# NaN-ignoring maximum of 65,536 rows: one in-place ScalarE pass in place of keys and write-backs

## The chip, the cores and the metric

The kernel runs on one core of one Trainium2 chip. The metric is device time in microseconds. A core has five engines with instruction queues of their own: TensorE (PE in the profile), VectorE (DVE), ScalarE (ACT), GpSimd (POOL) and SyncE (SP), which here only issues transfers. Transfers between the device memory and the on-chip memory (128 partitions) run on 16 DMA engines beside them. Engines wait for each other through semaphores.

## The reference

```python
def setup_inputs():
    batch, seq, dim = 32, 2048, 2048
    x = np.random.randn(batch, seq, dim).astype(np.float32)
    mask = np.random.rand(batch, seq, dim) < 0.1
    x[mask] = np.nan
    return {"x": x, "axis": -1}

def reference(x, axis):
    return np.nanmax(x, axis=axis).astype(np.float32)
```

There are 65,536 rows of 2,048 float32 values, 536.87 MB in all; a tenth of the values are NaN. Each row gives the largest of its values that are not NaN (NaN, if all are).

## The kernel before

Each of the 128 partitions holds 512 rows. The list `TILES` cuts them into 74 tiles; an entry gives the tile's loads, the pieces of ScalarE's pass and the widths of VectorE's reductions, in quarter rows of 512 values. The bulk of the list are tiles of 28 quarters (7 rows, 56 KB in each partition, 7,168 KB in all) fetched by one load; towards the end a tile comes in more and smaller loads. Three buffers `xt` are used in turn, and a load into a buffer waits for the last reduction of the tile that was in it. The loads are issued by SP, in order, each with one of 14 semaphores in turn.

[...]

- ScalarE reads the upper half-words of a piece of the tile (every second 16-bit element of `xt`) and writes a dense 16-bit key into one of three buffers `kt`: a `Prelu` of 32639.25 minus the half-word, whose slope on the negative side sends NaN to a key that comes back as minus infinity.
- The write-back computes 32639 minus the key and puts it into the upper half-words of `xt`, again every second 16-bit element. GpSimd does most pieces (a positive number in `TILES`), ScalarE the rest (a negative one).

VectorE then takes the maximum of each row from `xt` (`tensor_reduce` in float32; line 239 in the profile). A reduction may cover part of a row; its result is left in the tile, in the element before the next part, which takes it in. At the end `find` (VectorE) and `find_late` (GpSimd) turn rows that are still minus infinity into NaN, and SP stores the results of six groups of rows in six transfers.

The order of work on each engine is the order in which the program calls `order.add`, which attaches to each instruction the semaphore waits that its engine has not yet seen. The lines of the profile are those of the helpers: L222 is every activation of ScalarE, L232 every write-back of GpSimd, L239 every reduction, L316 the loads, L461 the stores, L245 `find`. The key pass and ScalarE's write-back share line 222, so they are told apart by what they read and write: `kt<-xt` is the key pass, `xt<-kt` the write-back.

Of the kernel before, what the change touches and what calls it, by code (L numbers as in the profile page):

```python
# [7 lines left out]
D = 2048  # L9

Q = D // 4

TILES = (
    [([4], [4], [4])]
    + [([28], [7, 9, 12], [16, 12])] * 7
    + [([28], [9, 12, -7], [8, 20])]
    + [([28], [7, 9, 12], [16, 12])] * 7  # L20
    + [([28], [9, 12, -7], [8, 20])]
    + [([28], [7, 9, 12], [16, 12])] * 7
    + [([28], [9, 12, -7], [8, 20])]
    + [([28], [7, 9, 12], [16, 12])] * 7
    + [([28], [9, 12, -7], [8, 20])]
    + [([28], [7, 9, 12], [16, 12])] * 7
    + [([28], [9, 12, -7], [8, 20])]
    + [([28], [7, 9, 12], [16, 12])] * 7
    + [([28], [6, 10, 12], [16, 12])] * 3
    + [([28], [7, 9, 12], [16, 12])]  # L30
    + [([28], [6, 10, 12], [16, 12])] * 3
    + [([28], [7, 9, 12], [12, 16])] * 2
    + [([28], [7, 10, 11], [12, 16])]
    + [([28], [6, 10, 12], [16, 12])] * 3
# [13 lines left out]
)  # L48

GROUPS = [TILES[i : i + 15] for i in range(0, 60, 15)] + [TILES[60:73], TILES[73:]]  # L50


FLAGGED = (3, 5)
LATE = 4

APART = (70, 71, 72, 73)
WIDE = 7
BUFS = 3

KEYS = 3 * D  # L60
NKEYS = 3

LEAD = 128

# [4 lines left out]
TOP = 0x7F7F  # L69
NAN = 0x7FC0  # L70
LOW = -128

EDGE = TOP + 0.25

LEAST = -(2.0**128 - 2.0**104)


def total(pieces):
    return sum(sum(map(abs, p)) if isinstance(p, tuple) else abs(p) for p in pieces)


def joints(pieces, reds):

    flat = []
    at = 0  # L90
    for step, parts in enumerate(pieces):
        for c in parts if isinstance(parts, tuple) else (parts,):

            flat.append((at, at + abs(c), c < 0, step + isinstance(c, float)))
            at += abs(c)
    needs = []
    done = 0
    for n in reds:
        over = [i for i, (a, b, _, _) in enumerate(flat) if a < done + n and b > done]
        done += n  # L100
        pools = [i for i in over if not flat[i][2]]
        backs = [i for i in over if flat[i][2]]
        if pools and backs and flat[pools[-1]][3] > flat[backs[-1]][3]:
            backs = []
        needs.append(pools[-1:] + backs[-1:])
    pairs = {}
    for need in needs:
        if len(need) == 2 and all(sum(i in n for n in needs) == 1 for i in need):
            for i in need:
                pairs[i] = tuple(need)  # L110
    return pairs


class Order:

# [18 lines left out]
    def unseen(self, who, deps):  # L134
        seen = self.seen.setdefault(who, {})
        return [(s, v) for s, v in deps if seen.get(s, 0) < v]

    def needed(self, who, deps):

        seen = self.seen.setdefault(who, {})  # L140
        want = {}
        for s, v in self.unseen(who, deps):
            want[s] = max(want.get(s, 0), v)
# [10 lines left out]
    def add(self, who, engine, issue, deps, lane=None, step=1, joint=False):  # L154
# [12 lines left out]
        past = self.past.get((name, event[1] - step), {}) if joint else {}  # L167
        self.past[event] = {**past, **self.seen[who], name: event[1]}
        return event
# [3 lines left out]
def kernel(  # L173
# [6 lines left out]

# [13 lines left out]
    ACT = mybir.ActivationFunctionType  # L194

# [7 lines left out]
    rows = [sum(sum(loads) for loads, _, _ in g) * Q // D for g in GROUPS]  # L203
    assert R == P * sum(rows)

    sing = ctx.enter_context(tc.tile_pool(name="sing", bufs=1))

    scalars = sing.tile([P, LEAD // 4], f32, name="scalars")
    warm = scalars[:, 1:2]
    xts = [sing.tile([P, WIDE * D], i32, name=f"xt{i}") for i in range(BUFS)]  # L210
    kts = [sing.tile([P, KEYS], u16, name=f"kt{i}") for i in range(NKEYS)]
    accs = sing.tile([P, sum(rows)], f32, name="acc")
    late = sing.tile([P, rows[LATE]], i32, name="late")

    with tc.tile_critical():  # L215
        order = Order(nc)

        def act(deps, pair=None, **kw):
            return order.add(
                "act",  # L220
                nc.scalar,
                lambda: nc.scalar.activation(**kw),  # L222
                deps,
                lane=pair,
                joint=pair is not None,
            )

        def pool(deps, pair=None, **kw):
            return order.add(
                "pool",  # L230
                nc.gpsimd,
                lambda: nc.gpsimd.tensor_scalar(**kw),  # L232
                deps,
                lane=pair,
                joint=pair is not None,
            )
# [4 lines left out]
        def find(deps, acc):  # L241
            return order.add(
                "dve",
                nc.vector,
                lambda: nc.vector.scalar_tensor_tensor(  # L245
                    out=acc,
                    in0=acc,
                    scalar=LEAST,
                    in1=acc,
                    op0=ALU.is_ge,  # L250
                    op1=ALU.mult,
                ),
                deps,
            )

        def find_late(deps, acc, none):
            e = order.add(
                "pool",
                nc.gpsimd,
                lambda: nc.gpsimd.tensor_scalar(  # L260
                    out=none,
                    in0=acc,
                    scalar1=LEAST,
                    scalar2=float(0x00400000),
                    op0=ALU.is_lt,
                    op1=ALU.mult,
                ),
                deps,
            )
            bits = acc.bitcast(i32)  # L270
            return order.add(
                "pool",
                nc.gpsimd,
                lambda: nc.gpsimd.tensor_tensor(out=bits, in0=bits, in1=none, op=ALU.add),  # L274
                [e],
            )

        e_warm = order.add("dve", nc.vector, lambda: nc.vector.memset(warm, 1.0), [])  # L278
        act([e_warm], out=warm, in_=warm, func=ACT.Prelu, alpha=0.5)

        free = [[] for _ in range(BUFS)]
        kfree = [[] for _ in range(NKEYS)]
        clock = 0

        def last(uses):

            return list({back: e for back, _, e in sorted(uses, key=lambda u: u[1])}.values())

        key = 0
        used = KEYS  # L290
        number = 0
        lanes = [[] for _ in range(LANES)]
        turn = 0
        stores = []
        ready = []
        flagged = 0
        r0 = 0
        for gi, (s, g) in enumerate(zip(rows, GROUPS)):
# [3 lines left out]
            first = sum(rows[:gi])  # L302
            acc = accs[:, first : first + s]
            base = 0
            for loads, pieces, reds in g:
                assert sum(loads) == total(pieces) == sum(reds)
                xt, before = xts[number % BUFS], free[number % BUFS]
                number += 1
                landed = []
                at = 0  # L310
                for c in loads:
                    c *= Q
# [191 lines left out]
```

## Time and profile before

| What | Value |
|---|---|
| Median of 3 runs | 1252.61 us (1252.61 to 1252.66) |
| Span of the profiled execution | 1250.7 us |
| VectorE busy | 1111.4 us, 179 instructions |
| ScalarE busy | 965.6 us, 273 instructions |
| GpSimd busy | 1168.5 us, 242 instructions |
| Read from device memory | 536.87 MB, 429 GB/s over the span |
| Loads | 105, of which 61 of 7,168 KB |
| ScalarE's key pass (`kt<-xt`) | 913.4 us in 247 instructions |
| ScalarE's write-back (`xt<-kt`) | 52.8 us in 24 |
| GpSimd's write-back (`xt<-kt`) | 1167.4 us in 236 |
| VectorE's reductions | 1109.2 us in 176 |

The profiled execution is one run of the program under the hardware profiler; the median comes from runs without it and is 1.9 us longer than the profile's span. In a list of groups, a row gives the line, the engine and the operation, then what it writes and reads with the shape (partitions by elements per partition), the count, the busy time in us and the mean of one in ns, and last the idle time of the engine just before these instructions and what ended it. In a timeline a row gives the start and the length in us; several like instructions in a row are merged, and the count stands behind the x. The DMA row gives the busy share of the 16 DMA engines in tenths, in 40 equal slices of the span or of the window; the GB/s row what they moved in each.

### The profile page before, as it was taken

To read this page: it belongs to the slowest core of one execution; us is meant where nothing else is said; L and a number is where in the kernel's file an instruction comes from. 1 tells how busy PE (TensorE), PEld (TensorE's weight loads), DVE (VectorE), ACT (ScalarE), POOL (GpSimd) and SP (SyncE) were. 2 spreads that over 40 slices of the span, in tenths; PEclk is the share of its full clock that TensorE was granted. 3 is DMA by queue.
4 is the path that set the end of the run, shared out by engine and by line. 5 is a ranking of instruction groups with operands and counts; after the bars stand their busy time and mean duration, and the time that the engine had idled before them with its cause. 6 is when DMAs were issued, how large, how long until landed. Compare 5 with 4: busy or idle time off the path is not lost.

```text
span 1250.7 us, 891 instructions
## 1 busy us (share of the span) xinstructions
DVE 1111.4 (89%) x179; ACT 965.6 (77%) x273; POOL 1168.5 (93%) x242
## 2 busy tenths in 40 slices
DVE  0888989888889888898988888998888899999999
ACT  3777887778777877788777877777777778999997
POOL 2999989998999899998999899999999999989998
DMA  9999999999999999999999999999999999999997
GB/s 415 440 418 433 440 440 438 413 440 440 440 433 418 440 440 438 429 424 440 440 436 424 431 440 438 436 424 433 440 438 435 422 436 436 425 434 429 431 428 301
DMA packets 15991, 537.20 MB, mean 430 GB/s; under 512 B 2544, under 2 KB 2544, under 8 KB 3568
## 3 DMA queue, kind: packets, MB, share of 16 engines
q1 hardware_dynamic: 15984, 537.14, 99.4%
q14 instruction: 7, 0.06, 0.0%
HBM read 536.87 MB, written 0.26 MB: 429 GB/s over the span
## 4 chain that ended last, share of the span: by engine, by line
DMA 40%; DVE 29%; POOL 22%; ACT 9%; issue 1%; SPq 0%
DMA xt<-in_x_dram 40%; DVE acc L239 29%; POOL xt L232 22%; ACT kt L222 8%; ACT xt L222 1%; SPq L316 0%; DVE acc L245 0%; SPq L499 0%; SPq L215 0%
## 5 line engine op out<-in xcount | busy, mean ns | idle before, releaser
L232 POOL TENSOR_SCALAR xt<-kt 128x3584 int16<-128x3584 uint16 (+11 forms) x236 | 1167.4, 4947 | 77.6 <-ACT kt L222 63.9
L239 DVE TENSOR_REDUCE acc<-xt 128x3 f32<-128x6144 f32 (+4 forms) x175 | 1107.5, 6379 | 135.6 <-POOL xt L232 128.1
L222 ACT ACTIVATE kt<-xt 128x3584 uint16<-128x3584 int16 (+9 forms) x247 | 913.4, 3734 | 278.0 <-DMA xt<-in_x_dram 257.9
L222 ACT ACTIVATE xt<-kt 128x512 int16<-128x512 uint16 (+6 forms) x24 | 52.8, 2202 | 0.7
L245 DVE SCALAR_TENSOR_TENSOR acc<-acc 128x414 f32<-128x414 f32 (+1 forms) x2 | 2.2, 1111 | 0.1
L222 ACT ACT_TABLE_LOAD x1 | 1.3, 1283 | 0.9 <-SPq L215 0.9
L239 DVE TENSOR_REDUCE xt<-xt 128x1 f32<-128x1536 f32 x1 | 1.7, 1743 | 0.0
L278 DVE MEMSET scalars<- 128x1 f32 x1 | 0.1, 59 | 1.0 <-SPq L215 1.0
L260 POOL TENSOR_SCALAR late<-acc 128x91 int32<-128x91 f32 x1 | 0.5, 549 | 0.1
L274 POOL TENSOR_TENSOR acc<-acc,late 128x91 int32<-128x91 int32 x1 | 0.3, 341 | 0.1
L485 POOL MEMSET const-float32-0.0<- 128x1 f32 x1 | 0.1, 98 | 0.2 <-issue 0.2
L222 ACT ACTIVATE scalars<-scalars 128x1 f32<-128x1 f32 x1 | 0.2, 203 | 0.0
L485 POOL MEMSET const-bfloat16-1.0<- 128x1 bf16 x1 | 0.1, 101 | 0.0
L485 POOL MEMSET const-uint8-127<- 128x1 uint8 x1 | 0.1, 101 | 0.0
L485 POOL MEMSET const-float32-1.0<- 128x1 f32 x1 | 0.1, 98 | 0.0
## 6 DMA issues: line engine op xcount, KB each, us to landing
xt<-in_x_dram SPq DMA_DIRECT2D x61, 7168.0 KB, 22.6
xt<-in_x_dram SPq DMA_DIRECT2D x2, 5120.0 KB, 17.4
xt<-in_x_dram SPq DMA_DIRECT2D x3, 2816.0 KB, 22.7
xt<-in_x_dram SPq DMA_DIRECT2D x4, 2048.0 KB, 22.3
xt<-in_x_dram SPq DMA_DIRECT2D x5, 1536.0 KB, 29.1
xt<-in_x_dram SPq DMA_DIRECT2D x2, 3584.0 KB, 24.8
xt<-in_x_dram SPq DMA_DIRECT2D x6, 1024.0 KB, 26.8
xt<-in_x_dram SPq DMA_DIRECT2D x3, 1792.0 KB, 30.1
```

What stands on the lines that cost most here:

```text
L222: lambda: nc.scalar.activation(**kw),
L232: lambda: nc.gpsimd.tensor_scalar(**kw),
L239: return order.add("dve", nc.vector, lambda: do(**kw), deps)
L245: lambda: nc.vector.scalar_tensor_tensor(out=acc, in0=acc, scalar=LEAST, in1=acc, op0=ALU.is_ge, op1=ALU.mult,),
L260: lambda: nc.gpsimd.tensor_scalar(out=none, in0=acc, scalar1=LEAST, scalar2=float(0x00400000), op0=ALU.is_lt, op1=ALU.mult,),
L274: lambda: nc.gpsimd.tensor_tensor(out=bits, in0=bits, in1=none, op=ALU.add),
L278: e_warm = order.add("dve", nc.vector, lambda: nc.vector.memset(warm, 1.0), [])
L485: nc = _bacc.Bacc("TRN2", target_bir_lowering=False, num_devices=1)
```

## The change

The two steps become one. ScalarE reads the upper half-words h of a piece of `xt` as signed 16-bit numbers and writes max(2h - 32640, 0), as an unsigned 16-bit number, into the same place. In this code NaN becomes the half-word of minus zero and every value under 2 becomes a number under the smallest normal one (2 to the power of -126), while values from 2 up keep their order, with the lower half-words as they are. VectorE takes the maxima as before. A decode of the upper half-words of the results, (code + 32640) / 2, gives the values back.

A row with no value of 2 or more has no normal number in the result. Such rows are marked on GpSimd (`mark`), the marks are summed (ScalarE, and TensorE over the partitions), the sum is loaded into a register on VectorE and ScalarE, and if it isn't zero, a general path (`general`) computes everything anew. The inputs here don't lead into it.

There are no keys, no buffers `kt` and no write-backs any more; GpSimd only marks and decodes. The tiles are cut anew, in units of 256 values: 52 tiles of 64 units (8 rows, 64 KB in each partition) in one load each, then 15 tiles of 24 to 64 units with loads that shrink to 3 to 5 units, 98 loads in all. A load of 24 units or more is passed over by ScalarE in two pieces, split at a row. The rows form two groups (501 and 11 rows in each partition) in place of six, so there are two stores.

```diff
-TILES = (
-    [([4], [4], [4])]
-    + [([28], [7, 9, 12], [16, 12])] * 7
...
+U = 256
+ROW = D // U
+TILES = [[64]] * 52 + [
+    [56],
+    [56],
+    [40],
+    [48],
+    [32, 32],
+    [40],
+    [26, 30],
+    [32],
+    [27, 29],
+    [16, 24],
+    [15, 17, 16, 16],
+    [15, 14, 12, 13, 10],
+    [11, 11, 10, 8, 8, 8, 8],
+    [8, 8, 7, 7, 6, 6, 6, 6, 5, 5],
+    [3, 5, 5, 3, 4, 4],
+]
...
+def pieces(load, at):
+    if load >= 3 * ROW:
+        half = (at + load // 2) // ROW * ROW - at
+        return [half, load - half]
+    return [load]
...
+        def decode(where, a, b, deps):
+            add, do = (dve, nc.vector) if where == "dve" else (pool, nc.gpsimd)
+            return add(
                 deps,
+                do.tensor_scalar,
+                out=halves[:, a:b],
+                in0=halves[:, a:b],
+                scalar1=float(INF),
+                scalar2=0.5,
+                op0=ALU.add,
+                op1=ALU.mult,
             )
...
+                if number == len(TILES) - 1:
+                    e_early = total(late[:, 0:1], low, [e_low])
...
-                        act(
-                            [e],
-                            name(i),
-                            out=xt[:, a:b].bitcast(i16)[:, 1::2],
-                            in_=kp,
-                            func=ACT.Copy,
-                            bias=float(TOP),
-                            scale=-1.0,
...
+                    for piece in pieces(load, at):
+                        span = xt[:, at * U : (at + piece) * U]
+                        e_clean = act(
                             [e],
+                            out=span.bitcast(u16)[:, 1::2],
+                            in_=span.bitcast(i16)[:, 1::2],
+                            func=ACT.Relu,
+                            bias=float(-INF),
+                            scale=2.0,
                         )
...
+                e = mark(late[:, 1:s], accs[:, first : S - 1], [e_before])
+                e_dec = decode("pool", first, S - 1, [e_before, e])
+                e = mark(late[:, s : s + 1], last_part, [e_part])
+                e_sums = order.add(
+                    "pe",
+                    nc.tensor,
+                    lambda: nc.tensor.matmul(sums, lhsT=ones, rhs=late, start=True, stop=True),
+                    [e, e_early, e_ones],
+                )
+                e = decode("dve", S - 1, S, [e_max])
...
+        e_sum = total(flag, sums, [e_sums])
+        order.wait("act", nc.scalar, [e_sum])
+        order.wait("dve", nc.vector, [e_sum])
+        lows = nc.values_load(
+            flag.bitcast(i32),
+            engines=[ENG.DVE, ENG.Activation],
+            skip_runtime_bounds_check_because="it is only compared with zero",
+        )
+        with nc.If(lows != 0):
+            general(nc, order, ended, xr, of, xts, accs, small)
```

More of the change, by code (lines that the diff above doesn't have):

```diff
@@ L50 @@
[L50 to L57, printed above, removed]
+U = 256
[17 more added lines that the diff above has]
+]
+SPLIT = len(TILES) - 2
+WIDE = 8
@@ L58 @@
 BUFS = 3
-KEYS = 3 * D
-NKEYS = 3
-LEAD = 128
 LANES = 14
[L69 to L111, printed above, removed]
+INF = 0x7F80
@@ L114 @@
+NORMAL = 2.0**-126
 class Order:
@@ L152, in needed, with wait, add @@
         return list(want.items())
-    def add(self, who, engine, issue, deps, lane=None, step=1, joint=False):
+    def wait(self, who, engine, deps):
+        for s, v in self.needed(who, deps):
+            engine.wait_ge(self.sems[s], v)
+    def add(self, who, engine, issue, deps, lane=None, step=1):
         want = self.needed(who, deps)
@@ L202 @@
     of = out.bitcast(i32).flatten_outer_dims().rearrange("r c -> (r c)")
-    rows = [sum(sum(loads) for loads, _, _ in g) * Q // D for g in GROUPS]
-    assert R == P * sum(rows)
+    groups = [TILES[:SPLIT], TILES[SPLIT:]]
+    rows = [sum(map(sum, g)) // ROW for g in groups]
+    S = sum(rows)
+    assert R == P * S
+    assert all(sum(t) % ROW == 0 and sum(t) <= WIDE * ROW for t in TILES)
     sing = ctx.enter_context(tc.tile_pool(name="sing", bufs=1))
-    scalars = sing.tile([P, LEAD // 4], f32, name="scalars")
@@ L209 @@
-    warm = scalars[:, 1:2]
+    psum = ctx.enter_context(tc.tile_pool(name="psum", bufs=1, space=bass.MemoryType.PSUM))
     xts = [sing.tile([P, WIDE * D], i32, name=f"xt{i}") for i in range(BUFS)]
-    kts = [sing.tile([P, KEYS], u16, name=f"kt{i}") for i in range(NKEYS)]
-    accs = sing.tile([P, sum(rows)], f32, name="acc")
-    late = sing.tile([P, rows[LATE]], i32, name="late")
+    accs = sing.tile([P, S], f32, name="acc")
+    low = sing.tile([P, rows[0]], f32, name="low")
+    late = sing.tile([P, 1 + rows[1]], f32, name="late")
@@ L215 @@
+    small = sing.tile([P, 64], f32, name="small")
+    sums = psum.tile([1, 1 + rows[1]], f32, name="sums")
+    ones, warm, flag = small[:, 0:1], small[:, 1:2], small[0:1, 2:3]
+    halves = accs.bitcast(u16)[:, 1::2]
     with tc.tile_critical():
         order = Order(nc)
[L218 to L236, printed above, removed]
+        def act(deps, **kw):
+            return order.add("act", nc.scalar, lambda: nc.scalar.activation(**kw), deps)
         def dve(deps, do, **kw):
             return order.add("dve", nc.vector, lambda: do(**kw), deps)
[L241 to L252, printed above, removed]
-                deps,
-            )
@@ L278, with pool @@
-        e_warm = order.add("dve", nc.vector, lambda: nc.vector.memset(warm, 1.0), [])
-        act([e_warm], out=warm, in_=warm, func=ACT.Prelu, alpha=0.5)
-        free = [[] for _ in range(BUFS)]
[L282 to L291, printed above, removed]
+        def pool(deps, do, **kw):
+            return order.add("pool", nc.gpsimd, lambda: do(**kw), deps)
@@ L301 @@
             r0 += P * s
-            first = sum(rows[:gi])
-            acc = accs[:, first : first + s]
             base = 0
-            for loads, pieces, reds in g:
-                assert sum(loads) == total(pieces) == sum(reds)
+            for loads in g:
                 xt, before = xts[number % BUFS], free[number % BUFS]
-                number += 1
-                landed = []
                 at = 0
-                for c in loads:
-                    c *= Q
+                part = []
+                if number == len(TILES) - 1:
+                    e_early = total(late[:, 0:1], low, [e_low])
+                for load in loads:
                     e = order.add(
@@ L324 @@
                     turn = (turn + 1) % LANES
-                    landed.append((at, at + c, e))
-                    at += c
-                clean = []
-                after = []
-                at = done = 0
-                reds = [n * Q for n in reds]
-                part = []
-                held = []
-                pairs = {}
-                if number not in APART:
-                    pairs = joints(pieces, [n // Q for n in reds])
-                flat = sum((p if isinstance(p, tuple) else (p,) for p in pieces), ())
@@ L441 @@
-                            after.append(e)
-                free[(number - 1) % BUFS] = after[-1:]
-                base += at
-            stores.append((og, acc.bitcast(i32)))
-            if gi == LATE:
-                late_after = after
-            elif gi not in FLAGGED:
-                continue
-            lo, flagged = flagged, first + s
-            if gi == LATE:
-                late_acc = accs[:, lo:flagged]
-            else:
-                e = find(after, accs[:, lo:flagged])
-                ready += [e] * (gi + 1 - len(ready))
@@ L455 @@
-            if gi == len(GROUPS) - 1:
-                ready[LATE] = find_late(late_after, late_acc, late)
-        for (og, bits), e in zip(stores, ready):
-            last = order.add(
-                "sp",
-                nc.sync,
-                lambda: nc.sync.dma_start(out=og, in_=bits),
-                [e],
-                lane="store",
-                step=16,
-            )
+                            part = [e_max]
+                            if row == S - 1 and b % ROW:
+                                last_part, e_part = to, e_max
@@ new lines @@
+            first += s
+        ended = []
+        for og, bits, deps in stores:
+            ended.append(
+                order.add(
+                    "sp",
+                    nc.sync,
+                    lambda: nc.sync.dma_start(out=og, in_=bits),
+                    deps,
+                    lane="store",
+                    step=16,
+                )
+            )
+        e_sum = total(flag, sums, [e_sums])
+        order.wait("act", nc.scalar, [e_sum])
+        order.wait("dve", nc.vector, [e_sum])
```

243 lines of the change are left out of this document (112 added, 131 removed), and 13 rows, old and new, of the table TILES.

## The prediction

> **What bounds the kernel now.** I read the page's busy shares and its 40 slices first, then the timeline of the steady part, the groups with shapes kept apart, the timeline of the last 11 us, and the DMA rates of two windows.
>
> ```profile
> DVE 1111.4 (89%) x179; ACT 965.6 (77%) x273; POOL 1168.5 (93%) x242
> ...
> DMA  9999999999999999999999999999999999999997
> ...
> q1 hardware_dynamic: 15984, 537.14, 99.4%
> ```
>
> No engine is full; the DMA row is, in every slice but the last. The loads are the bound, and what can be won lies in their length and in what follows them.
>
> ```profile
> 22.58 7.12 ACT L222 ACTIVATE kt<-xt 128x3584 uint16<-128x3584 int16 x2 [14.97 <-DMA xt<-in_x_dram]
> ...
> 39.48 7.12 ACT L222 ACTIVATE kt<-xt 128x3584 uint16<-128x3584 int16 x2 [4.10 <-DMA xt<-in_x_dram]
> ...
> 56.47 7.12 ACT L222 ACTIVATE kt<-xt 128x3584 uint16<-128x3584 int16 x2 [4.16 <-DMA xt<-in_x_dram]
> ```
>
> Each line is ScalarE starting on a tile that has just landed. Tiles of 7,168 KB (7,340,032 B) land every 16.9 us: (107.19 - 22.58) / 5 = 16.92 with a later line of the same view, so 433.8 GB/s.
>
> ```profile
> L239 DVE TENSOR_REDUCE acc<-xt 128x4 f32<-128x8192 f32 x57 | 495.1, 8686 | 114.1 <-POOL xt L232 114.1
> L232 POOL TENSOR_SCALAR xt<-kt 128x6144 int16<-128x6144 uint16 x61 | 429.7, 7044 | 6.0 <-ACT kt L222 1.3
> ...
> L222 ACT ACTIVATE kt<-xt 128x6144 uint16<-128x6144 int16 x61 | 324.6, 5321 | 17.2 <-POOL xt L232 17.1
> ...
> L222 ACT ACTIVATE kt<-xt 128x3584 uint16<-128x3584 int16 x57 | 181.8, 3189 | 182.0 <-DMA xt<-in_x_dram 180.8 <-POOL xt L232 1.2
> ...
> L239 DVE TENSOR_REDUCE acc<-xt 128x1 f32<-128x2048 f32 x29 | 64.2, 2276 | 9.1 <-POOL xt L232 9.1
> ...
> L222 ACT ACTIVATE xt<-kt 128x3584 int16<-128x3584 uint16 x5 | 21.0, 4201 | 0.2
> ...
> L222 ACT ACTIVATE xt<-kt 128x512 int16<-128x512 uint16 x6 | 4.7, 776 | 0.2
> ...
> L232 POOL TENSOR_SCALAR xt<-kt 128x512 int16<-128x512 uint16 x3 | 2.3, 761 | 0.2
> ```
>
> These give rates. ScalarE's key pass reads every second half-word of a tile and writes a dense buffer: (5321 - 3189) / 2560 = 0.833 ns per element. Its write-back reads densely and writes every second half-word: (4201 - 776) / 3072 = 1.115 ns, plus 205 ns. GpSimd's write-back, of the same pattern: (7044 - 761) / 5632 = 1.116 ns. Two engines with the same slope say that the write pattern costs it. VectorE: (8686 - 2276) / 6144 = 1.043 ns, plus 0.14 us.
>
> ```profile
> 1242.23 0.78 ACT L222 ACTIVATE xt<-kt 128x512 int16<-128x512 uint16 x1
> 1242.88 1.55 ACT L222 ACTIVATE kt<-xt 128x1024 uint16<-128x1024 int16 x2
> ...
> 1246.50 1.97 SPq L461 DMA_DIRECT2D out_dram<-acc  x2
> 1247.94 0.17 DVE L245 SCALAR_TENSOR_TENSOR acc<-acc 128x7 f32<-128x7 f32 x1
> ```
>
> Back to back, an instruction starts 0.13 us before the other ends (1242.23 + 0.78 against 1242.88). VectorE's last instruction ends at 1248.11; the last store and the end take 2.59 us to 1250.7.
>
> ```profile
> GB/s 416 441 416 416 429 429 410 413 416 419 460 441 403 422 410 432 403 444 444 416 425 397 444 435 321 199 60 2 0 0 0 0 0 0 72 0 3 2 13 0
> ```
>
> This is the window 1225 to 1251, 0.65 us a slice: the loads run dry at about 1242. The tail behind them is 8.7 us, of which VectorE's queue holds six.
>
> **The sum is made against the profiled 1250.7 us span**; the median of the runs is 1252.61, so 1.9 us are added at the end.
>
> **Loads.** The same 536.87 MB in 98 loads instead of 105, nothing new on SP's queue but two stores for six. In the window 1000 to 1240 the rate answered is 430 GB/s for 103.25 MB, 2.1 us more than at 433.8, over some 45 loads: 0.05 us each. Seven loads less are worth between 0 and 0.3 us; I keep 1242 as their end. An 8 MiB load then lands every 8,388,608 B / 433.8 = 19.34 us.
>
> **Removed.** 236 write-backs on GpSimd (1167 us), 24 on ScalarE (53 us), the keys' buffers, `find` and `find_late`. The steady part gains nothing, since the loads hide them all, and they hide the new pass too as long as ScalarE needs under 19.34 us for a tile. The first tile is now 8 MiB, so ScalarE begins at some 21.6 instead of 5.7 us; the 0.9 us that it waits in every tile (below) pays for that.
>
> **Added: the in-place pass.** It writes every second half-word of `xt`, as both write-backs do, and reads every second half-word, as the key pass does. No row has the two together. Bounds: 0.833 ns (strided writing costs nothing when the reading is strided too) and 1.115 + (1.115 - 0.833) = 1.40 ns (the reading of the same lines pays the same again). I take 1.115: the output access is literally that of the 1.115 row, and a strided read alone adds nothing in the 0.833 row. Between instructions I take 0.11 us of overlap (0.09 within the pair of key passes, 0.13 above), so 0.095 us remains of the 205 ns.
>
> Large tiles: 52 of 64 units (a unit is 256 elements, 128 KiB over all partitions), two instructions of 8,192 elements: 2 x (0.095 + 9.134) = 18.46 us. It fits into 19.34 with 5% to spare, and the tile is done 18.6 us after it landed. VectorE needs 2 x (8.55 + 0.05) = 17.2 us and is done some 27 us after landing; the buffer is wanted again after 2 x 19.34 = 38.7, so no load waits.
>
> The shrinking tiles: 768 units, 46 loads, 59 ScalarE instructions. Loads: 100.66 MB at 430 GB/s = 234.1 us. ScalarE: 768 x 256 x 1.115 ns = 219.2, 59 x 0.095 = 5.6, and the sum of flags put before the last tile (501 elements, 0.5): 225.3 us. It enters 18.6 us late and catches up by only 234.1 - 225.3 = 8.8, so it ends **9.8 us after the last load**, at 1251.8. At c ns per element the lag is 213 c - 227.7 us: zero at c = 1.069, and 2.1 us more for each 0.01 above.
>
> **After it.** VectorE's last reduction of 1,024 elements with its waits: 1.3 us, to 1253.1. Its decode of one column, 0.06 to 0.17 us (the 128x1 memset, the last `find`): 0.1. Store and end: 2.59. So 1255.8.
>
> **Added: the register load and the branch.** Flags go through GpSimd, a matmul and ScalarE into a register of VectorE and ScalarE; then both branch. The load waits behind ScalarE's last piece and VectorE's decode, beside the last store; behind it on both engines are only the branch and the barrier of the end, for which SP waits. GpSimd's marks and decode of the first 501 columns fall among the last 25 loads, where GpSimd has nothing else to do. GpSimd's 128x91 took 549 ns, its steps start from the last partial maximum, 1.3 us before the end, so this chain ends with the last reduction; only the register load stands behind. No row has one: 0 (hidden by the store's 1.41 us of issue and landing) to 1.4 (a round trip like that one, all of it late). I take 0.7, as the end's barrier takes part of the cover: 1256.5 us of span, **1258.5 us** with the 1.9.
>
> Where rule and row differ. The row for the same output access is 1.115 ns. The Trainium skill, page "ScalarE: Activation LUTs" (section "What ACT_TABLE_LOAD costs"), gives one element per cycle, 0.833 ns, for every function, and its page "SBUF — State Buffer" (section "Door 1", the note on cachelines) says that a stride of up to 8 bf16 elements is free. By that rule the pass would cost 0.833 ns and the sum would be rival A's; the trace agrees for the key pass and contradicts it for the write-back.
>
> **The rivals.**
>
> A. The in-place pass costs 0.833 to 1.07 ns: what is slow is not the strided write but a dense read together with one. For it: no row shows reading and writing at the same pace. Against it: equal slopes on two engines, and a dense read is the easier one. Then VectorE sets the tail. It enters the shrinking tiles 24.2 us late (half a tile on ScalarE, 6.9, then two reductions, 17.3), does 205.2 + 79 x 0.05 + 18 x 0.12 (pieces of a row that wait for the piece before) = 211.3 us in 234.1, and the last piece cannot end under some 3 us behind its load (ScalarE 1.1, two reductions): 1242 + 3.2 + 0.1 + 2.6 = 1247.9, and 0 to 1.4 for the register: a time of 1249.8 to 1251.2, less 0.3 for the loads and up to 0.8 should the last piece follow its load more closely (1.1 + 1.3): say 1250.0. It decides from c below 1.07.
>
> B. Read and write collide and c passes (19.34 - 0.19) / 16,384 = 1.169 ns. ScalarE is then the bound throughout, and loads wait for it. At 1.40 ns: 1,048,576 x 1.40 = 1468, 163 x 0.095 = 15.5, 21.6 before the first tile and 5.2 behind: about 1512 us. For it: the write-back's 0.28 ns shows that these accesses do cost. Against it: nothing in the trace slows when other engines use the same tile.
>
> C. The lag is right, but the release of buffers makes loads wait as well. VectorE ends 27 us after landing against 38.7: it costs nothing below c = 1.17. I give it no chance of its own.
>
> **How the numbers follow.** Forecast (c from 1.10 to 1.15; 1255.3 to 1266 by 2.1 us per 0.01): 0.51. A: 0.33. Between the two (c 1.07 to 1.10): 0.03. B, with c above 1.15: 0.13. A change of 0.2% (2.5 us, about what a measurement of this kernel can tell from none) puts A on the line at 1250.1: I split it 0.2 faster, 0.13 same, and add the 0.03 to the same. Slower: 0.51 + 0.13 = 0.64. Both signs are in play, so the range reaches from A's lower end, 1248.7, to 1266 and leaves out B alone. The forecast's own range: 1255.3 to 1266.
>
> **What would show it.** Right: the in-place ScalarE group at 128x8192 has a mean near 9.34 us; DMA stays at 9 until 1240; in the last 200 us ScalarE has no idle time and its last pass ends 9 to 11 us after the loads run dry; the chain ends in a long run of ScalarE, then VectorE. A shows as a mean of 7.0 us, ScalarE waiting for DMA to the end, and VectorE behind it. B shows as a mean over 9.6 us and DMA slices under 9 throughout. A register load over 1.4 us, or loads that move under 430 GB/s from rows 4.1 MB apart instead of 0.9, would make the prediction wrong from another side.

## The result, and the profile after

The changed kernel takes **1259.21 us** (median of 4 runs, 1258.59 to 1259.64) against 1252.63 us (1252.61 to 1252.7) for the kernel before: a ratio of 1.0052, 95% interval 1.0038 to 1.0066. It is slower by 6.6 us. The profiled execution is the one of 1259.64 us, the slowest of the four; its span is 1257.9 us, 7.2 us more than the 1250.7 of before.

Page of the changed kernel: busy time of the engines, DMA in 40 slices, the loads' queue, and the chain that ended last.

```profile
PE 0.2 (0%) x2; PEld 0.1 (0%) x2; DVE 1115.4 (89%) x186; ACT 1178.5 (94%) x169; POOL 3.1 (0%) x9
...
DMA  9999999999999999999999999999999999999996
...
q1 hardware_dynamic: 14400, 537.14, 99.1%
...
DMA 46%; ACT 35%; DVE 19%; issue 1%; SPq 0%; DVEq 0%
```

The chain of the kernel before:

```profile
DMA 40%; DVE 29%; POOL 22%; ACT 9%; issue 1%; SPq 0%
```

GpSimd has gone from 1168.5 us to 3.1, ScalarE from 965.6 to 1178.5. The DMA row still reads 9 in every slice but the last, so the loads are still the bound of the steady part; ScalarE has taken GpSimd's place in the chain that ended last, with 35% in place of the 9% that it had before. (The chain follows a load back to the release of its buffer even when other loads are still ahead of it in the queue, so these shares don't say that ScalarE binds the steady part.)

Groups of the changed kernel with shapes kept apart (count, then busy us, mean ns of one, idle us before and what ended it):

```profile
L230 ACT ACTIVATE xt<-xt 128x8192 uint16<-128x8192 int16 x106 | 974.0, 9252 | 70.9 <-DMA xt<-in_x_dram 70.9
L233 DVE TENSOR_REDUCE acc<-xt 128x4 f32<-128x8192 f32 x106 | 920.7, 8686 | 134.7 <-ACT xt L230 134.7
...
L230 ACT ACTIVATE xt<-xt 128x4096 uint16<-128x4096 int16 x14 | 65.0, 4710 | 1.3 <-DMA xt<-in_x_dram 1.3
```

The in-place pass costs (9252 - 4710) / 4096 = 1.109 ns per element, the rate of the write-backs that it replaces, and VectorE's 8686 ns is what it was. ScalarE waits for loads mainly in front of the full tiles: 20.8 us before the first, and about 1 us before each of the other 51; in the shrinking tiles it waits only 1.7 us in all.

Timeline of the end of the changed kernel (start, length; several instructions in a row are merged):

```profile
1244.44 7.22 ACT L230 ACTIVATE xt<-xt 128x768 uint16<-128x768 int16 x6
...
1253.83 1.22 DVE L233 TENSOR_REDUCE acc<-xt 128x1 f32<-128x1025 f32 x1
...
1255.09 0.16 DVE L233 TENSOR_SCALAR acc<-acc 128x1 uint16<-128x1 uint16 x1
1255.27 0.34 SPq L358 DMA_DIRECT2D out_dram<-acc  x1
```

ScalarE's pass ends at 1251.66, VectorE at 1255.25; before, VectorE ended at 1248.11. By the trace's landing times the last load is there at **1248.5 us, against 1242.2 before**. So of VectorE's 7.1 us, 6.3 lie in front of the last landing, although the same bytes are loaded in seven loads less, and only 0.8 behind it. That was not expected, and most of the experiments go to it. One place where the loads stood still is plain to see. Windows of the changed kernel (length; busy us of PE, PEld, DVE, ACT, POOL; clock, DMA share, GB/s):

```profile
1040.00:1060.00 20.00, 0.00 (x0) 0.00 (x0) 19.10 (x3) 20.00 (x3) 0.00 (x0) 1.00 0.99 419
1060.00:1080.00 20.00, 0.00 (x0) 0.00 (x0) 19.28 (x3) 19.64 (x5) 0.00 (x0) 1.00 0.94 384
1080.00:1100.00 20.00, 0.00 (x0) 0.00 (x0) 20.00 (x5) 20.00 (x5) 0.00 (x0) 1.00 1.01 434
```

Against the 433 GB/s of its steady part it loses 14 and 49 GB/s there. Much of the rest is spread over the whole span: a load with 64 KB in each partition lands every 19.35 us (below), where the rate of the kernel before would give 19.32.

### The profile page after: what moved, and what is told of

Same layout as the page of the kernel before. It is cut to its first block, busy times and chain, and to the rows that moved or that the text cites. A ratio compares the mean times of both kernels' runs of the same rounds, so it can differ in the third digit from the quotient of the medians.

```text
span 1257.9 us, 558 instructions
## 1 busy us (share of the span) xinstructions
PE 0.2 (0%) x2; PEld 0.1 (0%) x2; DVE 1115.4 (89%) x186; ACT 1178.5 (94%) x169; POOL 3.1 (0%) x9
## 4 chain that ended last, share of the span: by engine, by line
DMA 46%; ACT 35%; DVE 19%; issue 1%; SPq 0%; DVEq 0%
DMA xt<-in_x_dram 46%; ACT xt L230 35%; DVE acc L233 17%; DVE xt L233 2%; SPq L409 0%; DVEq L86 0%; SPq L226 0%
## 5 line engine op out<-in xcount | busy, mean ns | idle before, releaser
L230 ACT ACTIVATE xt<-xt 128x8192 uint16<-128x8192 int16 (+12 forms) x163 | 1176.3, 7302 | 72.5 <-DMA xt<-in_x_dram 72.5
L233 DVE TENSOR_REDUCE acc<-xt 128x4 f32<-128x8192 f32 (+8 forms) x165 | 1092.7, 6641 | 138.8 <-ACT xt L230 138.1
L233 DVE TENSOR_REDUCE xt<-xt 128x1 f32<-128x768 f32 (+6 forms) x18 | 23.9, 1328 | 0.0
```

The source lines that it names most:

```text
L230: return order.add("act", nc.scalar, lambda: nc.scalar.activation(**kw), deps)
L233: return order.add("dve", nc.vector, lambda: do(**kw), deps)
```

## The experiments

The theory to start with: the time is lost to ScalarE's pass at 1.11 ns per element, and the strided write makes it so. The main rival: the time is lost to the loads, through the larger rows, the greater pitch or the buffers.

### What the pass costs: dense writing, dense reading

The first run makes the write dense and keeps the strided read.

```diff
-                            out=span.bitcast(u16)[:, 1::2],
+                            out=span.bitcast(u16)[:, 0 : piece * U],
```

> ScalarE reads as in the changed kernel but writes its result densely, into the first half of the same piece; VectorE takes the maxima as integers, and the marks, the sum and the branch are left out. The output is not the reference's: the values are left in the wrong places. Theory (the strided write costs 1.108 ns per element, the read nothing): the group at 128x8192 falls from a mean of 9252 ns to about 7010 (190 + 0.833 x 8192), ScalarE waits for loads to the end, loads no longer wait for buffers in the shrinking tiles, VectorE sets the tail, and the time is 1252 (1250.5 to 1253.5), 7 us under the changed kernel. Rival (it is reading and writing in the same place that costs): the mean stays over 9 us and the time at 1258 to 1260.

Measured: 1253.45 us (1253.28 to 1253.68), ratio 1.0005 (0.9996 to 1.0015). Groups of that run:

```profile
L230 ACT ACTIVATE xt<-xt 128x8192 uint16<-128x8192 int16 x106 | 739.4, 7021 | 296.6 <-DMA xt<-in_x_dram 296.6
...
L230 ACT ACTIVATE xt<-xt 128x4096 uint16<-128x4096 int16 x14 | 50.1, 3606 | 12.2 <-DMA xt<-in_x_dram 12.2
```

That is (7021 - 3606) / 4096 = 0.834 ns per element. The second run is its counterpart, a dense read and the strided write.

```diff
-                            in_=span.bitcast(i16)[:, 1::2],
+                            in_=span.bitcast(i16)[:, piece * U : 2 * piece * U],
```

> The pass reads its input densely (the same number of 16-bit values, from the second half of each piece) and still writes every second 16-bit value; the maxima are taken as integers, and the sum, its register and the branch are left out; so the output is not the reference's. Theory (the strided write sets the pace of the pass): an instruction of 8192 elements stays at 9.25 us, and the time stays with that of the run without the sum, 1257.5 to 1259.5 us. Rival (the strided read has a share in it): the instruction falls to somewhere between 7.0 and 9.2 us, and ScalarE waits longer for its loads; at 7.0 us the time would be that of the dense write, 1253.5 us.

Measured: 1259.85 us (1258.56 to 1260.19), ratio 1.0053 (1.0038 to 1.0069), just above the range given.

```profile
L230 ACT ACTIVATE xt<-xt 128x8192 uint16<-128x8192 int16 x106 | 978.2, 9292 | 66.7 <-DMA xt<-in_x_dram 66.7
```

The instruction takes 9292 ns with a dense read and 9252 with a strided one. Writing every second half-word alone sets the pace; reading so costs nothing here. By the Trainium skill's page "SBUF — State Buffer" (section "Door 1", the note on cachelines) such a stride costs nothing; the runs agree for the read and contradict it for the write, 1.109 ns against 0.834.

A second thing follows: even with the fast pass the changed kernel doesn't come under the kernel before, because its last load lands at 1246.1 us, 3.9 us later than before. Something other than ScalarE delays the loads.

### The pitch of the rows, and the flags

Here the 52 full tiles go in blocks of 13, so that the rows of two partitions lie about 0.85 MB apart in device memory, as before, and not 4.1.

```diff
+    blocks = [TILES[i : i + 13] for i in range(0, SPLIT, 13)] + [TILES[SPLIT:]]
...
+                q0, q1, base = where[number]
+                xg = xr[q0 : q0 + P * q1].rearrange("(p s) d -> p (s d)", p=P)
```

> Only the rows are dealt out anew: blocks of 13 tiles, so that neighbouring partitions read rows 0.8 MB apart in place of 4.1 MB; all else as in the changed kernel, but six stores. Theory (the longer step between partitions costs 4.9 ns in every 64 KB descriptor): descriptors of 64 KB take 2417 ns in place of 2422, a 64 KB load lands every 19.32 us in place of 19.36, and the time falls by 1 to 2.5 us, to 1257.5, since ScalarE still sets the end of the shrinking tiles. Rival (ScalarE's strided traffic or the length of the loads costs it): 2422 ns and 1259.2 as before.

Measured: 1258.32 us (1258.2 to 1260.15), ratio 1.0044 (1.0027 to 1.0060). A descriptor is one partition's part of a load; its time stands in the trace's DMA packets, which no view lists one by one. Nine in ten of those of 65,536 bytes lie between 2418 and 2426 ns, as in the changed kernel (median 2420 against 2422, mean 2424 against 2423). The pitch isn't it; that theory fell.

The next run leaves out the marks, their sum, the register, the branch and the general path.

```diff
-                e_low = mark(low, accs[:, 0:s], [e_max])
...
-        lows = nc.values_load(
...
-        with nc.If(lows != 0):
-            general(nc, order, ended, xr, of, xts, accs, small)
```

> The marks, their sums, the register load, the branch and the general path are left out; the result is the same for these inputs. Theory (the register load is hidden beside the last store; only the sum of flags on ScalarE before the last tile lies on the path): 0.3 to 0.7 us less than the changed kernel, 1258.7. Rival (the register load and branch add their 0.5 us and what follows): 1.2 us less or more, under 1258.0.

Measured: 1258.19 us (1257.69 to 1259.54), ratio 1.0046 (1.0030 to 1.0063). That is 1.0 us under 1259.21, between what theory and rival gave, and the runs of the two kernels overlap, so the time doesn't decide. The traces do: VectorE's last instruction is followed by 2.6 us to the end of the span in the changed kernel, with all this left out, and in the kernel before (2.59). The register load lies beside the last store.

### Taking the bound off ScalarE: GpSimd does a part

GpSimd does the same operation on the first 8 units of each large piece, 2,048 elements, and ScalarE the rest.

```diff
+                        mine = ROW if piece >= 2 * ROW and load >= 3 * ROW else 0
...
+                                pool(
+                                    [e],
+                                    nc.gpsimd.tensor_scalar,
+                                    out=halfs[0][:, 0 : mine * U],
+                                    in0=halfs[1][:, 0 : mine * U],
+                                    scalar1=2.0,
+                                    scalar2=float(-INF),
+                                    op0=ALU.mult,
+                                    op1=ALU.add,
```

> Of every ScalarE piece of 16 units or more in a load of 24 or more, GpSimd does the first 8 units with the same code (its write turns negative numbers to 0); nothing else is changed. Theory (the end is the lag that ScalarE carries through the shrinking tiles): ScalarE needs 14.0 us for a large tile in place of 18.4, it waits for loads to the end, no load waits for a buffer, and the time falls by 5 to 6.5 us, to 1253.5 (1252.5 to 1254.5). Rival (the end is set by the loads, which land 6.3 us later than before, whatever ScalarE does): the last load still lands at 1248 and the time falls by less than 2 us.

Measured: 1254.85 us (1254.67 to 1255.0), ratio 1.0016 (1.0007 to 1.0026), 0.35 above the range. Waits and a group of that run:

```profile
ACT xt L230 <- DMA xt<-in_x_dram: 347.9, 68, 20.8
...
L236 POOL TENSOR_SCALAR xt<-xt 128x2048 uint16<-128x2048 int16 x125 | 304.1, 2465 | 857.3 <-DMA xt<-in_x_dram 857.3
```

ScalarE now waits 347.9 us for loads and is no bound at all, the loads no longer stand still around 1060 us, and yet the last load lands at 1246.9 and the kernel is 2 us slower than before. The next thing to look at is the rate of the descriptors.

### The address of the buffers

In the kernel before, a descriptor's length in bytes times 0.03676 ns plus 8 ns gives its time (a fit to the packets; 2116 ns for 57,344 B, and 96% of these take just that). In the changed kernel they spread from that time to about 9 ns above it, small ones too, and are about 4 ns longer in the mean. One difference is easily missed in the diff: before, a 128-byte tile of `scalars` was allocated ahead of the buffers, which in the built program start at bytes 16,640, 73,984 and 131,328 of a partition, all multiples of 256. In the changed kernel that tile is gone, and they start at 16,512, 82,048 and 147,584, each 128 past a multiple. The first run of this part puts 128 bytes back (the new tile also takes in `warm`, one column that is used at the start alone).

```diff
+    first_tile = sing.tile([P, 32], f32, name="lead")
     xts = [sing.tile([P, WIDE * D], i32, name=f"xt{i}") for i in range(BUFS)]
```

> The changed kernel with one 128-byte tile put ahead of the three data tiles, so that each data tile starts at a multiple of 256 bytes again, as it did in the kernel before (there a 128-byte tile of scalars stood first). Nothing else differs. Theory (address): a 65,536-byte descriptor takes 2417 ns in place of 2422 ns, as the kernel before's rate for 57,344 bytes would give, loads land every 19.32 us in place of 19.35, and about 784 descriptors on each DMA engine x 4.9 ns = 3.8 us of the loads' time is gone; of it 1 to 2.5 us reach the end, because the ScalarE and VectorE work behind the last loads stays: 1256.7 to 1258.2 us, 1257.3 the likeliest. Rival (size): the 4.9 ns belong to the 64 KB row and not to the address: 2422 ns stays, 1259.2 us.

Measured: 1257.69 us (1256.39 to 1258.64), ratio 1.0041 (1.0027 to 1.0055). 95% of the descriptors of 65,536 B take 2418 ns now, where they had spread from 2418 to 2426. In the chain of the changed kernel, one load in three is on the path:

```profile
108.32 30.91 DMA xt<-in_x_dram
...
166.37 30.91 DMA xt<-in_x_dram
```

and with the 128 bytes:

```profile
108.46 30.80 DMA xt<-in_x_dram
...
166.41 30.81 DMA xt<-in_x_dram
```

The starts of the two lines lie three loads apart: 58.05 / 3 = 19.35 us per load and 57.95 / 3 = 19.32. The counter-test takes the alignment from the kernel before.

```diff
-LEAD = 128
+LEAD = 256
```

> The kernel before with its leading tile of scalars made 256 bytes long in place of 128, so that its three data tiles start 128 bytes off a multiple of 256, as the changed kernel's do. Nothing else differs. Theory (address): its 57,344-byte descriptors, 2116 ns before, take about 4 to 5 ns longer, and since the loads never stand still in this kernel and set its end, some 61 x 8 x 4.5 ns for the large loads and as much per descriptor for the small ones, 3 to 4.5 us, come through: 1255.7 to 1257.3 us. Rival (the address matters to 64 KB rows only): 2116 ns stays and the time with it, 1252.7 us.

Measured: 1256.27 us (1256.0 to 1256.52) against 1252.74 (1252.54 to 1252.91), ratio 1.0028 (1.0018 to 1.0039). Its 57,344-byte descriptors have a median of 2121 ns in place of 2116, and its last load lands at 1246.2 us. They are not all alike: of 7,808, 1,619 still take 2116 ns, and most of the others 2118, 2121 or 2125. Summed over the descriptors of one DMA engine (105 loads x 8), the excess over the fit is 4.30 us, against 0.83 in the kernel before: 3.5 us more, and 3.5 us is what the run lost. The keys and the results move by the 128 bytes too, but no engine works at another pace for it (ScalarE's key pass of 6,144 elements takes 5321 ns in both, GpSimd's write-back 7043 and 7044). So the address of the loads is worth 3.5 us to this kernel, whose loads are its bound. One shift of 128 bytes was tried, in both directions; other offsets were not.

The Trainium skill, page "DMA: Bandwidth & Descriptors" (section "How a descriptor splits into AXI transactions"), says that a descriptor that doesn't start at a multiple of 256 B begins with a transaction from the boundary below, whose unused bytes still cost beats of 32 B. An estimate by that page: 128 unused bytes are 4 beats, and at the trace's 2418 ns for 65,536 B a beat takes 1.18 ns, so 4.7 ns; the median descriptor shows 4 to 5. Why some take no more and others 9 ns more stays open. The page says it of bytes that are fetched; here it is the address written to that moved.

### Buffers that come free too late

The 98 loads of the changed kernel land 3.5 us late in all at two of them, which begin the fourth and fifth tile after the full ones: 1.56 us at the 56th (48 units) and 1.94 at the 57th (32 units). A tile's buffer is wanted again when the next two tiles have come. At 0.302 us per unit that is 38.7 us for full tiles, but 96 units or 29.0 us for the fourth tile of the descending list 56, 56, 40, 48, 32+32, and 88 units or 26.6 us for the fifth, while VectorE is done only 27.1 us after a full tile has landed (139.23 to 166.36 in the chain), and 26.2 and 25.2 us after the two tiles of 56 units whose buffers are wanted here. What is left is too little: the 57th was issued at 1069.4 and landed at 1084.1, 14.7 us later, though its 32 units take only 9.7. The DMA packets of the trace show the first engines at work on it 1.0 us after the issue, but all 16 only some 4 us after it. Other sizes of the same sum:

```diff
-    [56],
-    [56],
-    [40],
-    [48],
+    [48],
+    [56],
+    [48],
+    [48],
```

> The changed kernel with four tile sizes changed: 48, 56, 48, 48 units after the 52 full tiles in place of 56, 56, 40, 48 (the same sum). Theory (buffers come free too late in the drop from 64 to 40 units, which cost the loads 3.5 us of standing still): the two gaps at loads 56 and 57 shrink to about 1 us together, and 1.7 us of the 2.3 us come through at the end: 1257.0 to 1258.0 us, 1257.5 the likeliest. Rival (the end is set by ScalarE's and VectorE's work behind the last loads, whenever these land): 1259.2 us.

Measured: 1257.69 us (1257.49 to 1257.72), ratio 1.0039 (1.0025 to 1.0052). Windows of this run, the same as above:

```profile
1040.00:1060.00 20.00, 0.00 (x0) 0.00 (x0) 18.42 (x4) 20.00 (x4) 0.00 (x0) 1.00 1.00 433
1060.00:1080.00 20.00, 0.00 (x0) 0.00 (x0) 20.00 (x4) 20.00 (x4) 0.00 (x0) 1.00 1.00 431
```

The dip is gone, the last load lands at 1246.0, and the scatter between runs goes from about 1 us to 0.2. Both repairs together:

> The changed kernel with both small changes, the 128-byte tile ahead of the data tiles and the four tile sizes 48, 56, 48, 48. Alone, each came to 1257.69 us. Theory (the two costs are separate, and the loads are earlier by their sum, 3.2 us from the address and 2.5 us from the gaps; ScalarE, which then lags the loads by more, gives about a third of it back): 3.2 to 4.2 us under the changed kernel's 1259.2, 1255.0 to 1256.0 us. Rival (both act on the same wait, or ScalarE's rate already sets the end): no better than either alone, 1257.0 to 1257.7 us. In neither case does it come under the kernel before.

Measured: 1255.96 us (1255.88 to 1256.07), ratio 1.0026 (1.0016 to 1.0036), at the upper edge of the theory's range. Timeline of its end:

```profile
1240.69 7.22 ACT L231 ACTIVATE xt<-xt 128x768 uint16<-128x768 int16 x6
...
1251.33 0.16 DVE L234 TENSOR_SCALAR acc<-acc 128x1 uint16<-128x1 uint16 x1
```

Now the last load lands at 1242.7, within 0.5 us of the kernel before, and what remains is the tail: ScalarE's pass ends 5.2 us after it (1247.91) and VectorE 8.8 us after it (1251.49). Before, VectorE ended 5.9 us after the last landing. So of the 6.6 us about half, 1259.21 - 1255.96 = 3.3, are the loads' (address and buffers), and the other half is what ScalarE's slower pass puts behind them. Taken in the other order the halves differ: GpSimd's share alone, with the address as it was, brought 1259.21 - 1254.85 = 4.4 us, and it ended the standing still too.

### GpSimd's share with the 128 bytes, and VectorE's queue

GpSimd's share and the 128 bytes in one kernel:

> GpSimd takes the first 8 units of each large piece, as in the earlier run (1254.85 us), and the 128-byte tile stands ahead of the data tiles. Theory (address): no engine is behind the loads here, so the whole gain of the loads but what the taper gives back comes through, 2 to 3.5 us: 1251.5 to 1253.0 us, level with the kernel before (1252.6). Rival (size): 1254.85 us again.

Measured: 1252.33 us (1252.21 to 1252.42) against 1252.78 (1252.53 to 1252.95), ratio 0.9996 (0.9987 to 1.0005): level. The last load lands at 1243.7 and VectorE ends 4.3 us later. To shorten that, GpSimd took half of each small piece as well:

```diff
-                        mine = ROW if piece >= 2 * ROW and load >= 3 * ROW else 0
+                        mine = ROW if piece >= 2 * ROW and load >= 3 * ROW else piece // 2
```

> As the run with GpSimd's share and the 128-byte tile ahead (1252.33 us), and GpSimd takes half of every piece of the small loads as well. Theory (behind the last load only ScalarE's and VectorE's work on the small pieces is left, 4.3 us there; halving the pass on a piece of 4 units saves ScalarE 0.6 us, and VectorE, which was behind ScalarE, can start earlier all through the last 90 us): 0.8 to 1.8 us less, 1250.5 to 1251.5 us, the first version under the kernel before. Rival (VectorE's queue sets the end whatever is ahead of it, since 18 of its reductions wait for the one before): 1252.3 us again.

Measured: 1254.63 us (1254.5 to 1254.9), ratio 1.0016 (1.0007 to 1.0025): 2.3 us slower, against theory and rival. Timeline of that run:

```profile
1220.02 1.49 POOL L237 TENSOR_SCALAR low<-acc 128x501 f32<-128x501 f32 x1 [3.11 <-DVE acc L234]
...
1221.60 0.76 POOL L237 TENSOR_SCALAR acc<-acc 128x501 uint16<-128x501 uint16 x1
1222.43 5.52 POOL L237 TENSOR_SCALAR xt<-xt 128x1024 uint16<-128x1024 int16 x5
...
1223.79 4.48 DVE L234 TENSOR_REDUCE acc<-xt 128x1 f32<-128x2048 f32 x2 [3.86 <-POOL xt L237]
```

GpSimd's queue is in order: `mark` on the first group waits 3.11 us for VectorE's last maximum of that group, then mark and decode take 2.3 us. Five pieces lie behind them, of which two had landed by then; GpSimd does the five in one stretch, all late. VectorE in turn waits 3.86 us for the first of these. So the two operations were moved behind GpSimd's third piece of the next tile:

```diff
+                    if number == SPLIT and i == 3:
+                        e_low = mark(low, accs[:, 0:first], [e_group])
+                        e = decode("pool", 0, first, [e_group, e_low])
```

> As the run in which GpSimd takes half of every small piece too (1254.63 us), but GpSimd's two operations on the 501 rows of the first group are put behind its third piece of the next tile, in place of ahead of that tile. Theory (in that run GpSimd stood 3.1 us for VectorE's last maximum of the group and worked 2.3 us on the rows, its next five pieces came late, and VectorE, which from there on is never idle, stood still for 3.86 us): the 3.86 us go, and most of them come through: 1250.5 to 1251.5 us. Rival (VectorE's 3.86 us only give back what it had gained, and its queue of small maxima sets the end): 1252.3 us, as without the small pieces.

Measured: 1251.78 us (1251.61 to 1252.1) against 1252.83 (1252.55 to 1252.93), ratio 0.9992 (0.9983 to 1.0001). The wait shrinks to 1.10 us:

```profile
1227.28 0.42 DVE L234 TENSOR_REDUCE acc<-xt 128x1 f32<-128x257 f32 x1 [1.10 <-POOL xt L237]
```

Of the 3.86 us, 2.85 came through, which ends 0.3 us above the range given. The runs of the two kernels don't overlap, but the interval of the ratio still touches 1: this is the best version found, about 1 us under the kernel before, and 7.4 us under the changed kernel.

## Why the prediction was right

The forecast was 1258.5 us; 1259.21 was measured, inside the forecast's own range. The mechanism is the one it named: the pass goes at the pace of the strided write, ScalarE falls behind in the shrinking tiles, and the end is set by ScalarE and then VectorE. That the total came within 0.7 us is luck: by the prediction's own steps most terms were off, and the errors cancel (+6.5, -6.6, +2.2 and -0.7 us in the table).

| Step | Predicted | Measured |
|---|---|---|
| In-place pass, ns per element | 1.115 | 1.109 |
| An 8,192-element instruction | near 9.34 us | 9.252 us |
| Last load landed | 1242 | 1248.5 |
| ScalarE's pass ends after it | 9.8 us | 3.2 us |
| VectorE ends after that | 1.4 us | 3.6 us |
| Register load and branch | 0.7 us | 0 |
| Span | 1256.5 | 1257.9 |

(The span of 1256.5 and the 1.9 us added to it make 1258.4; the prediction wrote 1258.5.) ScalarE's part of the profile shows why the errors cancel. Timeline of ScalarE alone, from the last full tile on:

```profile
1010.40 61.72 ACT L230 ACTIVATE xt<-xt 128x8192 uint16<-128x8192 int16 x8 [0.98 <-DMA xt<-in_x_dram]
1072.47 32.16 ACT L230 ACTIVATE xt<-xt 128x6144 uint16<-128x6144 int16 x6 [0.36 <-DMA xt<-in_x_dram]
1105.94 138.03 ACT L230 ACTIVATE xt<-xt 128x4096 uint16<-128x4096 int16 x41 [1.31 <-DMA xt<-in_x_dram]
```

From 1010.40 us on, ScalarE stands for only 0.36 + 1.31 = 1.7 us, so its end depends on the landing of the last full tile and on these two waits, and not on when the last load lands. It enters 2.5 us later than predicted (1242 - 234.1 = 1007.9), waits 1.7 us and works 239.6 us in place of 18.6 + 225.3 = 243.9, and so ends at 1251.7, where the prediction had 1251.8.

- **The pass.** The choice of 1.115, from the row with the same output access, was right, and so was the reason, that the write costs it. Its two ends fell: 0.833 (the dense write alone does that) and 1.40 (the strided read adds nothing).
- **The loads' end** is the term that was mis-sized, by 6.3 us. "I keep 1242 as their end" counted loads and bytes and neither the address of the buffers nor their release. The address: between the runs with GpSimd's share the last load moves from 1246.88 to 1243.74 with the 128 bytes, 3.1 us. The standing still around 1060 us: 1248.5 against 1246.0 with the even sizes, 2.5 us. About 0.6 us, the rest, lies at the start: the first 8,388,608 B have landed at 23.17 us, in the kernel before, where they come as two loads, at 22.55. No run tests why.
- **Rival C**, that releases make loads wait, got no chance of its own, and it happened. "Wanted again after 2 x 19.34 = 38.7" holds between full tiles only; where the list drops from 56 to 40 units it is 26.6 us, of which the work on the tile of 56 units took 25.2, and a load issued so late landed 5 us later than its own length asks for.
- **The lag of ScalarE.** With the loads' delays repaired it is 5.2 us rather than 9.8. There ScalarE, never idle from 1008.60 us on, needs 18.4 us for the last full tile and 220.9 for the shrinking ones, where 225.3 were predicted. Of the 4.4 us, 1.2 are the rate (196,608 elements x 0.006 ns); the rest is what an instruction costs besides its elements: 4709 - 4096 x 1.109 = 167 ns less some 0.13 of overlap, so 0.04 us in place of 0.095, 59 times. The 205 ns had been carried over from the write-back's rows. In the changed kernel itself the loads are so much later that the lag behind them is only 3.2, and the sign of being right "its last pass ends 9 to 11 us after the loads run dry" did not come.
- **VectorE's tail** was taken as one reduction. In the timeline its queue of small maxima is never idle in the last 10 us: it ends 3.6 us behind ScalarE, and the last reduction is 1.22 of these.
- **The register load** was given 0.7 of 0 to 1.4 us; 0 was right, it lies beside the store: the 2.6 us behind VectorE's last instruction are the same without it.
- **Rival A's time** was wrong in itself: 1250.0 us for a pass at 0.833 ns, where the run with the dense write gave 1253.45. It took the same end of the loads, which there came at 1246.1. Had the pass been fast, the forecast would have leaned to "faster" for a kernel that is level.
- **Rival B** didn't come about: at 1.109 ns a large tile takes 18.38 us of the 19.35 between landings.

## What to carry to other kernels

Where a kernel is bound by its loads, its small allocations are part of its timing: a tile of scalars that is dropped moves every buffer behind it, and 128 bytes cost the kernel before 3.5 us of 1252. Cost a pass by the access pattern that is the slowest in it, the strided write, and let a second engine take a share before trading it away. When tiles shrink, check the release of buffers against the next two tiles and not against the full ones, and put waits on another engine's last result behind the work that doesn't need them.

One premise is not tested: both kernels clean the NaNs out ahead of VectorE's maximum, and no run here shows what that maximum makes of a NaN.

## What the runs showed of the hardware that was not expected

- Descriptors whose destination starts 128 bytes past a multiple of 256 take 4 to 5 ns longer by their median, 2121 against 2116 ns at 57,344 B and 2422 against 2418 at 65,536 B, and spread over some 9 ns where the others nearly all take the same time.
- On ScalarE a write to every second 16-bit element costs 1.109 to 1.115 ns per element whether the read is dense or strided, in place or not; with a dense write it is 0.834.
- GpSimd's arithmetic of the same access takes 2462 to 2465 ns for 2,048 elements, about what ScalarE takes (2460), and it hardly slowed ScalarE (6998 ns for 6,144 elements, 6981 without it) and didn't slow VectorE (8681 ns, 8686 without).
